# A two-layer decoder trunk on one core: the weights as pairs of half units, twelve Strassen blocks, and the four sums of a block in one buffer

## The chip, the cores and the metric

The kernel runs on one core of a Trainium2 chip. The metric is the device time of one execution in microseconds (us), taken as the median of several runs. Before the change it is 943.9 us.

The core's engines work in parallel, each through its own list of instructions in order: TensorE (PE) multiplies, VectorE (DVE) and ScalarE (ACT) do elementwise work, GpSimd (POOL) and SyncE (SP) here mostly issue transfers (DMAs) from the chip's memory into the core's buffers. An instruction starts when the ones ahead of it on its engine are issued and the results that it needs have been signalled.

## The reference, cut to what matters

Two layers on 256 tokens of width 1024, all in float32. Each has a mixing half and an MLP half; the change concerns the weights of both and the work of the MLP half.

```python
for l in range(2):
    u = rms_norm(h, norm_mix_pre[l])
    q, k, v, xr, yr, pp, gt = split(u @ w_in[l])
    ...                               # attention, recurrence, pooling, gates
    h = h + rms_norm(merged @ w_out[l], norm_mix_post[l])
    m = rms_norm(h, norm_mlp_pre[l])
    y = square(relu(m @ w_mlp_up[l])) @ w_mlp_down[l]     # 1024 -> 4096 -> 1024
    h = h + rms_norm(y, norm_mlp_post[l])
```

## The kernel before, in words

**Split products.** PE multiplies in a format that holds fewer bits than float32. So each float32 operand is split into a high and a low part (`split`, lines L88 to L91: ACT makes the high part by a copy, DVE the low part by a subtraction), and `mm3` (L97 to L100) adds three products: high by high, high by low, low by high. In names, an `h` at the end is a high part and an `l` a low one: `wh` and `wl` of a weight unit, `dh`/`dl`, `sh`/`sl` and `bh`/`bl` of a Strassen block's weights.

**The weight stream.** All weights lie in memory as units of 128 rows by 1024 columns (512 KB) in the order of use. `load_to` has SP load them into a pool of seven buffers (`raws`), `split_to` splits them into the pools `his` and `los` of eight buffers each, `take` hands them to the matmuls. What a buffer's next load waits for is the last reader of what is in it, mostly DVE's subtraction.

**The MLP.** The hidden width of 4096 is cut into 16 blocks of 256. `up(j)` makes a block's hidden values (48 matmuls of 128x256), with ACT doing relu and square (L767, L768). The first ten blocks of a layer are multiplied with `w_mlp_down` by Strassen's scheme: a 2x2 by 2x2 block product with 7 instead of 8 products, each three matmuls of 128x512 (`down`). For this a block's down weights, four tiles of 512 columns here called b12, b21, b11, b22, are used alone (b12, b21 and b22) and in four sums t1 to t4. The sums t1 and t2 come by two POOL transfers (`dma_sums`): L794 brings two tiles into `dsum`, L796 adds a third onto both while it writes. A `dsum` buffer holds the sums of two blocks, there are two such buffers, and `dma_sums` is called for two blocks at a time. DVE makes t3 and t4 from them (L811, L812 in `weight_sums`) in a buffer `t34` of the `raws` pool. `weight_forms` splits t1/t2 and t3/t4 (`sh`, `sl`); `hidden_forms` makes the sums of the hidden values (`sm`, L778 to L781) and their split `xf`. The other six blocks of a layer (`PLAIN`) go without Strassen.

**What sets the order.** The order on each engine is that in which the Python code emits the instructions, but for a few calls that are put ahead by a priority. In the MLP loop `UPS[j]` says how many `up` steps stand in round j, before or in the `down` of block j. `ORDER` does this for the mixing half; `later(RGD, ...)` puts the gates of the recurrence (`rnn_gates`) off by RGD ticks.

Of the kernel before, what the change touches and what calls it, by code (L numbers as in the profile page):

```python
# [9 lines left out]
F32 = mybir.dt.float32  # L10
F32R = mybir.dt.float32r
# [5 lines left out]
L = 2  # L17
D = 1024
T = 256
# [2 lines left out]
EPS = 1e-6  # L22
WINDOWS = (2, 4, 8, 16)
HU_COLS = 1024
HP = 200
WARM = 12
NRAW = 7
NTMP = 28
NHI = 8
MID = 1  # L30
CST = 6
# [27 lines left out]
def trunk(ctx, tc, x, wts, rgw, par, gpost, eye, ctab, out):  # L59
# [6 lines left out]
    los = ctx.enter_context(tc.tile_pool(name="los", bufs=8))  # L66
# [12 lines left out]
    def ttile(shape, dt=F32, nm="t"):  # L79
        return tmp.tile(shape, dt, tag="t", name=nm)  # L80
# [7 lines left out]
    def split(hi, lo, src, scale=None):  # L88
        if scale is None:
            A.activation(hi, src, AF.Copy)  # L90
            V.tensor_tensor(out=lo, in0=src, in1=hi.bitcast(F32), op=ALU.subtract)  # L91
        else:
            A.activation(hi, src, AF.Copy, scale=scale)
            V.scalar_tensor_tensor(out=lo, in0=src, scalar=scale, in1=hi.bitcast(F32),
                                   op0=ALU.mult, op1=ALU.subtract)
# [29 lines left out]
    for i in range(WARM):  # L125
        PE.matmul(wps[:], warm[:, 0:P], warm[:], start=True, stop=True)


    NHU = wts.shape[0]
    st = {"load": 0, "split": 0, "use": 0}  # L130
    raw_t, hu_t = {}, {}

    nstr = NBLK - PLAIN
    pair_at = [[(l + 1) * (NHU // L) - 64 + 6 + 2 * j + 2 * (sum(UPS[:j - 1]) + 1 if j else 0) for j in range(nstr)]
               for l in range(L)]
    half = {i + 1 for at in pair_at for i in at}

    per_layer = NHU // L
    fine = {i + l * per_layer for l in range(L) for i in [*range(FINE[0]), *range(per_layer - 64, per_layer - 64 + FINE[1])]}

    def load_to(n):
        while st["load"] < min(n, NHU):
            i = st["load"]
            r = raws.tile([P, HU_COLS], F32, tag="raw", name=f"raw{i}")
            if i in half:
                nc.sync.dma_start(r[:, 512:1024], wts[i][:, 512:1024])
            else:
                nc.sync.dma_start(r[:], wts[i])
            raw_t[i] = r
            st["load"] += 1  # L150

    def split_to(n):
        while st["split"] < min(n, NHU):
            i = st["split"]
            load_to(i + 1)
            r = raw_t.pop(i)
            wh = his.tile([P, HU_COLS], F32R, tag="wh", name=f"wh{i}")
            wl = los.tile([P, HU_COLS], F32R, tag="wl", name=f"wl{i}")
            parts = 2 if i in fine else 1
            for k in range(parts):  # L160
                sl = slice(k * HU_COLS // parts, (k + 1) * HU_COLS // parts)
                split(wh[:, sl], wl[:, sl], r[:, sl])
            hu_t[i] = (wh, wl)
            st["split"] += 1
        load_to(n + NRAW - 1)

    def take(n):
        split_to(st["use"] + n)
        r = [hu_t.pop(st["use"] + i) for i in range(n)]
        st["use"] += n  # L170
        return r
# [118 lines left out]
    def new_normed(nm):  # L290

        t = acts.tile([P, 2, NC_, T], F32R, tag="both", name=nm, bufs=1)
        return t[:, 0], t[:, 1], t
# [65 lines left out]
        to_features(tt, u, prm[:, l, PG_PRE:PG_PRE + 8], uh, ul)  # L359

    uh, ul, u2 = new_normed("u")
    load_to(2)
    nc.sync.dma_start(h[:, 1, :], x[P:T, :])
    un = [mix_norm(0)]
    split_to(1)
    to_features(0, un[0], prm[:, 0, PG_PRE:PG_PRE + 8], uh, ul, between=lambda: split_to(2))
    split_to(3)
    load_to(CST)
    nc.sync.dma_start(cst[:], ctab)
    un.append(mix_norm(1))  # L370

    for l in range(L):
# [326 lines left out]
                {"pp": unit_pp, "pg": unit_pg, "yr": unit_yr, "xr": unit_xr}[kind](j)  # L699


        gB = gpool.tile([P, D], F32, tag="g", name="gB")
        nc.sync.dma_start(gB[:], gpost[l, 0])
        mix = [[bank([P, 512]) for _ in range(2)] for _ in range(2)]
# [26 lines left out]

        gB = gpool.tile([P, D], F32, tag="g", name="gB2")
        nc.sync.dma_start(gB[:], gpost[l, 1])
        prods, t8s = {}, {}
        zs, forms, wforms = {}, {}, {}

        def up_first():

# [46 lines left out]
            split(f[:, 0, 3:7, :], f[:, 1, 3:7, :], sm[:])  # L785
            forms[j] = f

        def dma_sums(j0):


            t = acts.tile([P, 2, 2, 512], F32, tag="lo", name="dsum")
            js = range(j0, min(j0 + 2, nstr))
            for j in js:
                nc.gpsimd.dma_start(t[:, j - j0], wts[pair_at[l][j]].rearrange("p (b n) -> p b n", b=2))  # L794
            for j in js:
                nc.gpsimd.dma_start(t[:, j - j0], wts[pair_at[l][j] + 1][:, 0:512].unsqueeze(1).to_broadcast([P, 2, 512]),  # L796
                                    accum_op=ALU.add)
                t8s[j] = t[:, j - j0]

        def weight_sums(j):  # L800

            load_to(st["split"] + 2)
            assert st["split"] == pair_at[l][j]
            r0, r1 = raw_t.pop(st["split"]), raw_t.pop(st["split"] + 1)
            st["split"] += 2
            st["use"] += 2
            t12 = t8s.pop(j)
            t34 = raws.tile([P, 2, 512], F32, tag="raw", name="t34")
            w1 = (his.tile([P, HU_COLS], F32R, tag="wh", name="dh"), los.tile([P, HU_COLS], F32R, tag="wl", name="dl"))
            w4 = (ttile([P, 512], F32R, nm="bh"), ttile([P, 512], F32R, nm="bl"))  # L810
            V.tensor_tensor(out=t34[:, 0, :], in0=t12[:, 0, :], in1=r0[:, 512:1024], op=ALU.add)  # L811
            V.tensor_tensor(out=t34[:, 1, :], in0=t34[:, 0, :], in1=r1[:, 512:1024], op=ALU.add)  # L812
            split(w1[0][:], w1[1][:], r0[:])
            split(w4[0][:], w4[1][:], r1[:, 512:1024])
            wforms[j] = [w1, w4, (t12, t34)]
            load_to(st["split"] + NRAW - 2)

        def weight_forms(j):
            for t in wforms[j].pop():
                w = (his.tile([P, HU_COLS], F32R, tag="wh", name="sh"), los.tile([P, HU_COLS], F32R, tag="wl", name="sl"))  # L820
                split(w[0][:], w[1][:], t.rearrange("p b n -> p (b n)"))
                wforms[j].append(w)

        def down(j, part):
            f = forms[j]
            w1, w4, w2, w3 = wforms[j]
            lo_, up_ = slice(0, 512), slice(512, 1024)

            for p, blk, w, cs in ((1, 2, w1, up_), (3, 6, w1, lo_), (2, 0, w4, lo_), (7, 5, w2, lo_), (5, 3, w2, up_),
                                  (6, 4, w3, lo_), (4, 1, w3, up_))[part]:  # L830
# [3 lines left out]
                mm3(prods[p][:], f[:, 0, blk, :], f[:, 1, blk, :], w[0][:, cs], w[1][:, cs], first, last)  # L834

        dma_sums(0)
        up_first()
        dma_sums(2)
        split_to(st["use"] + 2)
        up(2)  # L840
        weight_sums(0)
        split_to(st["use"] + 2)
        weight_forms(0)
        hidden_forms(0)
        nup = 3
        for j in range(nstr):
            if j % 2 and j + 3 < nstr:
                dma_sums(j + 3)
            for i in range(UPS[j]):
                up(nup)  # L850
                nup += 1
                if i == 0 and j + 1 < nstr:
                    weight_sums(j + 1)
                    hidden_forms(j + 1)
                if nup < NBLK:
                    split_to(st["use"] + 2)
# [103 lines left out]
def _layout(i):  # L960
    qc = np.concatenate([np.arange(hd * 64, hd * 64 + 64) for hd in _HEADS])
    units, rg, par, gp = [], [], [], []
    for l in range(L):
# [20 lines left out]
        pairs = [np.stack([np.concatenate([d[c][:, 512:], d[1 - c][:, :512]], 1) for c in range(2)]) for d in dn]  # L984
        units += [_s_units(i["w_mlp_up"][l][:, 0:512])[0], up[2], pairs[0], up[3]]
        nup = 3
        for j in range(nstr):
            for n in range(UPS[j]):
                nup += 1
                if n == 0 and j + 1 < nstr:  # L990
                    units.append(pairs[j + 1])
                if nup < NBLK:
# [14 lines left out]
    f = np.ascontiguousarray  # L1007
    return {
        "x": f(i["x"].reshape(T, D)),
        "wts": f(np.concatenate(units, 0)),  # L1010
        "rgw": f(np.stack(rg)),
        "par": f(np.stack(par, 1)),
        "gpost": f(np.array(gp)),
# [15 lines left out]
```

## Time and profile before

| | us |
|---|---|
| median of 3 runs (lowest, highest) | 943.9 (943.8, 944.44) |
| the profiled execution, its own time | 944.59 |
| its span from the first to the last instruction | 942.8 |
| granted TensorE clock, mean | 0.998 |
| PE busy | 932.3 |
| DVE busy, ACT busy | 750.0, 630.9 |

The rows of a timeline give the start in us, the duration in us, the engine, the line of the kernel, the operation, what it writes and reads, and in brackets how long its engine had been idle ahead of it and what ended that. Grouped rows give the count after an x, then the total in us and the mean in ns. Matmuls are pipelined, so that the distance from one start to the next tells their cost better than the duration of one; for DVE and ACT too, the next instruction may start a little before the last has ended. In the windows of busy time each engine has its busy us and its number of instructions.

### The profile page before, as it was taken

The numbers are of one execution on the slowest core, as the hardware profiler recorded it, in microseconds if no ns is written. First come the engines' busy times: TensorE is split into PE (matmuls) and PEld (weight loads), VectorE is DVE, ScalarE is ACT, GpSimd is POOL, SyncE is SP. The second block draws the span as 40 slices with busy tenths as digits, with TensorE's granted clock in tenths as the row PEclk, the third lists the DMA queues.
The fourth block names the chain that finished last, engine by engine and source line by source line (L and its number), as shares of the span: only waits on it lengthen the run. The fifth ranks groups of instructions, "written<-read, shape, count | busy, mean of one in ns | idle before, by whom it ended". The sixth has DMA issues, their size and how long they took to land.

```text
span 942.8 us, 14266 instructions
## 1 busy us (share of the span) xinstructions
PE 932.3 (99%) x5176; PEld 798.7 (85%) x5176; DVE 750.0 (80%) x1341; ACT 630.9 (67%) x1091; POOL 37.7 (4%) x60
## 2 busy tenths in 40 slices
PE   8999999999999999999999999999999999999997
PEld 5888987888888999998878888888888889999985
DVE  6878886878967987988596788776898598888963
ACT  8665765679837786767475666656896478767741
POOL 0000000000010111100000000000000101110000
PEclk9999999999999999999999999999999999999999
DMA  8765445544776888858457544645438688987621
GB/s 318 277 211 164 157 157 172 191 136 153 239 253 174 271 244 259 257 187 261 136 184 252 171 153 161 197 141 190 162 113 293 180 248 247 269 249 234 225 88 44
DMA packets 57062, 188.96 MB, mean 200 GB/s; under 512 B 6048, under 2 KB 6432, under 8 KB 56992
## 3 DMA queue, kind: packets, MB, share of 16 engines
q1 hardware_dynamic: 48384, 166.92, 52.6%
q0 software_dynamic: 8320, 20.97, 9.9%
q8 instruction: 40, 0.66, 0.3%
q14 instruction: 30, 0.25, 0.1%
q10 hardware_dynamic: 288, 0.17, 0.1%
HBM read 186.99 MB, written 1.05 MB: 199 GB/s over the span
## 4 chain that ended last, share of the span: by engine, by line
PE 98%; ACT 1%; DMA 1%; DVE 0%; issue 0%; SPq 0%; DVEq 0%
PE ps L98 18%; PE ps L99 17%; PE ps L100 17%; PE ps L304 9%; PE ps L341 9%; PE pr L98 6%; PE pr L99 6%; PE pr L100 6%; PE ps L306 5%; PE ps L429 1%; PE ps L477 1%; PE ps L466 1%; PE ps L230 1%; DMA raw<-wts 1%; PE ps L409 0%; PE ps L660 0%
## 5 line engine op out<-in xcount | busy, mean ns | idle before, releaser
L91 DVE TENSOR_TENSOR wl<-raw,wh 128x1024 fp32r<-128x1024 f32 (+1 forms) x304 | 333.5, 1123 | 67.0 <-ACT wh L90 57.7
L90 ACT ACTIVATE wh<-raw 128x1024 fp32r<-128x1024 f32 (+1 forms) x304 | 287.5, 987 | 127.1 <-PE ps L100 49.7
L98 PE MATMUL ps<-m,wh 128*128 128x256 f32 x448 | 126.9, 283 | 0.0
L100 PE MATMUL ps<-m,wl 128*128 128x256 f32 x448 | 126.9, 283 | 0.0
L99 PE MATMUL ps<-m,wh 128*128 128x256 f32 x448 | 126.9, 283 | 0.0
L304 PE MATMUL ps<-u,wh 128*128 128x512 f32 x384 | 96.9, 394 | 0.0
L99 PEld LDWEIGHTS ps<-m,wh 128*128 128x128 f32 x448 | 86.0, 192 | 1.0
L98 PEld LDWEIGHTS ps<-m,wh 128*128 128x128 f32 x448 | 86.0, 192 | 1.0
L100 PEld LDWEIGHTS ps<-m,wl 128*128 128x128 f32 x448 | 86.0, 192 | 0.0
L304 PEld LDWEIGHTS ps<-u,wh 128*128 128x128 f32 x384 | 69.5, 189 | 13.6 <-issue 0.7
L98 PE MATMUL ps<-wh,u 128*128 128x512 f32 x200 | 78.7, 393 | 0.8 <-ACT u L236 0.8
L100 PE MATMUL ps<-wh,u 128*128 128x512 f32 x200 | 78.0, 390 | 0.4 <-DVE u L238 0.4
L99 PE MATMUL ps<-wl,u 128*128 128x512 f32 x200 | 78.1, 391 | 0.0
L306 PEld LDWEIGHTS ps<-u,wl 128*128 128x128 f32 x384 | 52.4, 191 | 3.8
L306 PE MATMUL ps<-u,wl 128*128 128x256 f32 x384 | 53.5, 282 | 0.0
L98 PEld LDWEIGHTS ps<-wh,u 128*128 128x128 f32 x200 | 37.6, 188 | 9.3 <-ACT u L236 1.0
L100 PEld LDWEIGHTS ps<-wh,u 128*128 128x128 f32 x200 | 37.6, 188 | 8.6 <-DVE u L238 0.9
L99 PEld LDWEIGHTS ps<-wl,u 128*128 128x128 f32 x200 | 37.6, 188 | 7.7 <-DVE wl L91 0.4
L341 PE MATMUL ps<-wh,u 128*128 128x512 f32 x176 | 43.3, 394 | 0.0
L448 ACT ACTIVATE pr<-ps,s 128x128 f32<-128x128 f32 (+1 forms) x64 | 25.9, 430 | 25.8 <-DVE s L439 21.3
L341 PEld LDWEIGHTS ps<-wh,u 128*128 128x128 f32 x176 | 32.4, 188 | 7.9 <-ACT wh L90 0.9
L98 PE MATMUL pr<-wh,hid 128*128 128x512 f32 x96 | 37.5, 390 | 0.0
(234 smaller groups left out, 1992.5 us busy)
## 6 DMA issues: line engine op xcount, KB each, us to landing
raw<-wts SPq DMA_DIRECT2D x296, 512.0 KB, 4.6
dsum<-wts POOLq DMA_DIRECT2D x40, 512.0 KB, 6.9
raw<-wts SPq DMA_DIRECT2D x20, 256.0 KB, 5.0
gB<-gpost SPq DMA_DIRECT2D x4, 512.0 KB, 6.9
rg<-rgw SPq DMA_DIRECT2D x8, 256.0 KB, 4.4
out<-h SPq DMA_DIRECT2D x4, 256.0 KB, 2.0
h<-x SPq DMA_DIRECT2D x2, 256.0 KB, 3.3
h<-x SPq DMA_DIRECT2D x1, 512.0 KB, 7.1
```

What stands on the lines that cost most here:

```text
L90: A.activation(hi, src, AF.Copy)
L91: V.tensor_tensor(out=lo, in0=src, in1=hi.bitcast(F32), op=ALU.subtract)
L98: PE.matmul(o, lh, rh, start=start, stop=False, **kw)
L99: PE.matmul(o, lh, rl, start=False, stop=False, **kw)
L100: PE.matmul(o, ll, rh, start=False, stop=stop, **kw)
L230: PE.transpose(banks[c // 4][:, c % 4, :], src[c // 4][:, (c % 4) * P:(c % 4 + 1) * P], ident)
L304: PE.matmul(ps[:], ws[0][c], x2[:, :, c, :], start=c == 0, stop=False)
L306: PE.matmul(ps[:, 0, :], ws[1][c], x2[:, 0, c, :], start=False, stop=c == 7)
L341: PE.matmul(o, xx[:, c, tsl], ww[c], start=(n == 0 and c == 0), stop=(n == 2 and c == 7))
L429: PE.matmul(sc[hd // hp][:, hd % hp, :], qT[a, j // 2][rows, j % 2, blk * P:(blk + 1) * P], kTs[0][rows, a, 0:w], start=True, stop=True)
L448: A.activation(pr[:, j, :], sc[i][:, j, :], AF.Exp, bias=negm[:, hd:hd + 1], accum_out=sums[:, hd:hd + 1])
L466: PE.transpose(ps[:, g, :], g8["p"](4 * b + g)[:, kt * P:(kt + 1) * P], ident)
```

## The change

- A load is now 128 rows by 2048 columns (1 MB): two units side by side. `raws` has four buffers, `his` and `los` four of 2048 columns each. In the MLP a pair is split by one ACT and one DVE instruction of 2048 columns, in the mixing half by two of 1024, and by four of 512 for the first four pairs of a layer and of its MLP.
- A Strassen block's weights are one such row, of which three tiles of 512 columns (b12, b21 and b22 of the list above, 1536 columns) are loaded by SP and split as one piece.
- Twelve instead of ten blocks of a layer go by Strassen, four instead of six without; two `up` steps stand in the first round only.
- The four sums of a block lie in one buffer of 2048 columns: t1 and t2 by POOL's two transfers (now L726 and L727), t3 and t4 added behind them by DVE (now L823, L824). The buffer holds one block, and there are two. They are split as one piece of 2048 columns. `dma_sums(j + 3)` comes after `weight_forms(j + 1)`, and that of the first block ahead of the layer's output projection.
- `rnn_gates` is put off by six ticks instead of four. One temporary buffer fewer (27), and the loads at the program's start are called in pairs.

The core of the diff:

```diff
-NRAW = 7
-NTMP = 28
-NHI = 8
+PU_COLS = 2 * HU_COLS
+NRAW = 4
+NTMP = 27
+NHI = 4
-RGD = 4
-FINE = (8, 8)
-PLAIN = 6
+RGD = 6
+FINE = (4, 4)
+PLAIN = 4
-UPS = (2, 1, 1, 2, 1, 1, 2, 1, 1, 1)
+UPS = (2, 1, 1, 1, 1, 1, 1, 1, 1, 1, 1, 1)
...
+    def split_pair():
+        i = st["split"]
+        load_to(i + 1)
+        r = raw_t.pop(i)
+        wh = his.tile([P, PU_COLS], F32R, tag="wh", name=f"wh{i}")
+        wl = los.tile([P, PU_COLS], F32R, tag="wl", name=f"wl{i}")
+        n = 4 if i in fine else 2 if i % per_layer < per_layer - 32 else 1
...
+        def dma_sums(j):
+            t = acts.tile([P, PU_COLS], F32, tag="lo", name="dsum")
+            w = wts[pair_at[l][j]]
+            t2 = t[:, 0:1024].rearrange("p (b n) -> p b n", b=2)
+            nc.gpsimd.dma_start(t2, w[:, 0:1024].rearrange("p (b n) -> p b n", b=2))
+            nc.gpsimd.dma_start(t2, w[:, 1536:2048].unsqueeze(1).to_broadcast([P, 2, 512]), accum_op=ALU.add)
+            t8s[j] = t
...
         def weight_sums(j):
+            r = raw_t.pop(st["split"])
+            t = t8s[j]
+            V.tensor_tensor(out=t[:, 1024:1536], in0=t[:, 0:512], in1=r[:, 512:1024], op=ALU.add)
+            V.tensor_tensor(out=t[:, 1536:2048], in0=t[:, 1024:1536], in1=r[:, 1024:1536], op=ALU.add)
+            wh = his.tile([P, PU_COLS], F32R, tag="wh", name="dh")
+            wl = los.tile([P, PU_COLS], F32R, tag="wl", name="dl")
+            split(wh[:, 0:1536], wl[:, 0:1536], r[:, 0:1536])
...
         def weight_forms(j):
-            for t in wforms[j].pop():
-                w = (his.tile([P, HU_COLS], F32R, tag="wh", name="sh"), los.tile([P, HU_COLS], F32R, tag="wl", name="sl"))
-                split(w[0][:], w[1][:], t.rearrange("p b n -> p (b n)"))
+            t = t8s.pop(j)
+            wh = his.tile([P, PU_COLS], F32R, tag="wh", name="sh")
+            wl = los.tile([P, PU_COLS], F32R, tag="wl", name="sl")
+            split(wh[:], wl[:], t[:])
...
-            if j % 2 and j + 3 < nstr:
-                dma_sums(j + 3)
             for i in range(UPS[j]):
                 up(nup)
...
             if j + 1 < nstr:
                 weight_forms(j + 1)
+                if j + 3 < nstr:
+                    dma_sums(j + 3)
```

**What moves on DVE.** DVE's rows of one block in the middle of layer 0's MLP; the number in a name tells one buffer's use from another's. Before:

```order
L91 TENSOR_TENSOR bl_3991<-raw125_3836,bh_3990 128x512
L778 TENSOR_TENSOR sm_4000<-z_3561 128x128
L780 TENSOR_TENSOR sm_4000<-sm_4000,z_3561 128x128
L811 TENSOR_TENSOR t34_4110<-dsum_3748,raw128_3914 128x512
L812 TENSOR_TENSOR t34_4110<-t34_4110,raw129_3916 128x512
L91 TENSOR_TENSOR dl_4112<-raw128_3914,dh_4111 128x1024
L91 TENSOR_TENSOR xf_4005<-sm_4000,xf_4005 128x512
L91 TENSOR_TENSOR wl130_4134<-raw130_3998,wh130_4133 128x1024
L91 TENSOR_TENSOR wl131_4138<-raw131_4018,wh131_4137 128x1024
L91 TENSOR_TENSOR sl_4169<-dsum_3748,sh_4168 128x1024
L91 TENSOR_TENSOR sl_4173<-t34_4110,sh_4172 128x1024
```

After:

```order
L823 TENSOR_TENSOR dsum_3682<-dsum_3682,raw65_3685 128x512
L92 TENSOR_TENSOR dl_3846<-raw65_3685,dh_3845 128x1536
L824 TENSOR_TENSOR dsum_3682<-dsum_3682,raw65_3685 128x512
L92 TENSOR_TENSOR xf_3856<-z_3528,xf_3856 128x384
L806 TENSOR_TENSOR sm_3851<-z_3528 128x128
L808 TENSOR_TENSOR sm_3851<-sm_3851,z_3528 128x128
L92 TENSOR_TENSOR wl66_3862<-raw66_3745,wh66_3861 128x2048
L92 TENSOR_TENSOR sl_3887<-dsum_3682,sh_3886 128x2048
L92 TENSOR_TENSOR xf_3856<-sm_3851,xf_3856 128x512
```

The adds that read POOL's sums stand first in a block now, `wl` and `sl` are one row each, and the `xf` of the hidden sums comes behind `sl`.

**What moves on POOL.** The transfers of the sums in layer 0. Before:

```order
L794 DMA dsum_3061<-wts 128x1024 x2
L796 DMA dsum_3061<-wts 128x2x512 x2
L794 DMA dsum_3166<-wts 128x1024 x2
L796 DMA dsum_3166<-wts 128x2x512 x2
L794 DMA dsum_3497<-wts 128x1024 x2
L796 DMA dsum_3497<-wts 128x2x512 x2
```

After:

```order
L726 DMA dsum_3256<-wts 128x1024
L727 DMA dsum_3256<-wts 128x2x512
L726 DMA dsum_3370<-wts 128x1024
L727 DMA dsum_3370<-wts 128x2x512
L726 DMA dsum_3474<-wts 128x1024
L727 DMA dsum_3474<-wts 128x2x512
```

Each buffer is filled for one block by one transfer of either kind, where it was filled for two blocks by two.

**What moves on SP.** The weight loads in the same stretch. Before:

```order
L148 DMA raw124_3816<-wts 128x1024
L146 DMA raw125_3836<-wts 128x512
L148 DMA raw126_3838<-wts 128x1024
L148 DMA raw127_3840<-wts 128x1024
L148 DMA raw128_3914<-wts 128x1024
L146 DMA raw129_3916<-wts 128x512
```

After:

```order
L148 DMA raw59_3373<-wts 128x1536
L148 DMA raw60_3433<-wts 128x2048
L148 DMA raw61_3477<-wts 128x1536
L148 DMA raw62_3537<-wts 128x2048
L148 DMA raw63_3581<-wts 128x1536
```

Four loads per block have become two, of 1 MB for an `up` and of 768 KB for a Strassen block.

More of the change, by code (lines that the diff above doesn't have):

```diff
@@ L126, in trunk @@
         PE.matmul(wps[:], warm[:, 0:P], warm[:], start=True, stop=True)
-    NHU = wts.shape[0]
+    NHU = 2 * wts.shape[0]
     st = {"load": 0, "split": 0, "use": 0}
-    raw_t, hu_t = {}, {}
+    raw_t, hu_t, second = {}, {}, []
+    per_layer = wts.shape[0] // L
     nstr = NBLK - PLAIN
-    pair_at = [[(l + 1) * (NHU // L) - 64 + 6 + 2 * j + 2 * (sum(UPS[:j - 1]) + 1 if j else 0) for j in range(nstr)]
+    pair_at = [[(l + 1) * per_layer - 32 + 4 + j + (sum(UPS[:j - 1]) + (j == 1) if j else 0) for j in range(nstr)]
@@ L135, in trunk @@
                for l in range(L)]
-    half = {i + 1 for at in pair_at for i in at}
-    per_layer = NHU // L
-    fine = {i + l * per_layer for l in range(L) for i in [*range(FINE[0]), *range(per_layer - 64, per_layer - 64 + FINE[1])]}
+    three = {i for at in pair_at for i in at}
+    fine = {i + l * per_layer for l in range(L) for i in [*range(FINE[0]), *range(per_layer - 32, per_layer - 32 + FINE[1])]}
     def load_to(n):
-        while st["load"] < min(n, NHU):
+        while st["load"] < min(n, NHU // 2):
@@ L143, in load_to @@
             i = st["load"]
[L144 to L148, printed above, removed]
+            r = raws.tile([P, PU_COLS], F32, tag="raw", name=f"raw{i}")
+            n_ = 1536 if i in three else PU_COLS
+            step = HU_COLS if i < 2 else n_
+            for c in range(0, n_, step):
+                nc.sync.dma_start(r[:, c:c + step], wts[i][:, c:c + step])
@@ L149, in load_to, with pieces @@
             raw_t[i] = r
             st["load"] += 1
-    def split_to(n):
[L153 to L165, printed above, removed]
+    def split_pair():
[5 more added lines that the diff above has]
+        n = 4 if i in fine else 2 if i % per_layer < per_layer - 32 else 1
+        def pieces(ks):
+            for k in ks:
+                sl = slice(k * PU_COLS // n, (k + 1) * PU_COLS // n)
+                split(wh[:, sl], wl[:, sl], r[:, sl])
+        if i == 0:
+            pieces(range(2))
+            second.append(lambda: pieces(range(2, 4)))
+        else:
+            pieces(range(n))
+        for k in range(2):
+            sl = slice(k * HU_COLS, (k + 1) * HU_COLS)
+            hu_t[2 * i + k] = (wh[:, sl], wl[:, sl])
+        st["split"] += 1
@@ L167, in take @@
+    def split_to(n):
+        while 2 * st["split"] < min(n, NHU):
+            split_pair()
+        load_to((n + 1) // 2 + NRAW - 1)
     def take(n):
+        while st["use"] // 2 in three:
+            st["use"] += 2
         split_to(st["use"] + n)
@@ L361, in trunk @@
     uh, ul, u2 = new_normed("u")
+    load_to(1)
+    nc.sync.dma_start(h[:, 1, :], x[P:T, :])
     load_to(2)
[L363 removed]
     un = [mix_norm(0)]
     split_to(1)
[L366 to L368 removed]
+    to_features(0, un[0], prm[:, 0, PG_PRE:PG_PRE + 8], uh, ul, between=second[0])
+    split_to(4)
+    load_to(3)
     nc.sync.dma_start(cst[:], ctab)
@@ L786, in hidden_forms @@
             forms[j] = f
[L788 to L798, printed above, removed]
@@ L800, in weight_sums @@
         def weight_sums(j):
-            load_to(st["split"] + 2)
+            load_to(st["split"] + 1)
             assert st["split"] == pair_at[l][j]
[L804 to L809, printed above, removed]
@@ new lines, in weight_sums @@
+            st["split"] += 1
+            t = t8s[j]
[4 more added lines that the diff above has]
+            split(wh[:, 0:1536], wl[:, 0:1536], r[:, 0:1536])
+            wforms[j] = [(wh[:, i * 512:(i + 1) * 512], wl[:, i * 512:(i + 1) * 512]) for i in range(3)]
@@ L851, in trunk @@
                 nup += 1
+                if j == 0 and i == 0:
+                    split_pair()
                 if i == 0 and j + 1 < nstr:
```

47 lines of the change are left out of this document (21 added, 26 removed).

## The prediction

> **What bounds the kernel now.** I read the page first: the span, the busy time of the engines, the chain that ended last and the DMA queues.
>
> ```profile
> span 942.8 us, 14266 instructions
> PE 932.3 (99%) x5176; PEld 798.7 (85%) x5176; DVE 750.0 (80%) x1341; ACT 630.9 (67%) x1091; POOL 37.7 (4%) x60
> PE 98%; ACT 1%; DMA 1%; DVE 0%; issue 0%; SPq 0%; DVEq 0%
> q1 hardware_dynamic: 48384, 166.92, 52.6%
> q0 software_dynamic: 8320, 20.97, 9.9%
> ```
>
> TensorE (PE) works 99% of the span and carries 98% of the chain, so time can be won only by taking matmuls away, and lost only where something makes PE wait. Windows over the Strassen stage of layer 0 show that nothing does there now (PE, PEld, DVE, ACT, POOL, granted clock, DMA share, GB/s):
>
> ```profile
> 340.00:360.00 20.00, 20.00 (x134) 18.41 (x133) 17.98 (x28) 14.32 (x20) 3.53 (x4) 1.00 0.88 278
> 360.00:380.00 20.00, 20.00 (x136) 18.54 (x135) 15.52 (x22) 13.96 (x19) 2.34 (x3) 1.00 0.87 240
> ```
>
> PE is busy 20.00 of 20.00 us, but DVE 15.5 to 18.0 and the DMA engines 0.87 to 0.88: both have little to spare if their work is put in another order. The chain of waits gives the beat of a block, from the first matmul of one `down` to that of the next:
>
> ```profile
> 349.90 0.23 PE pr L98
> 354.46 0.23 PE pr L100
> 360.44 0.23 PE pr L98
> ```
>
> A block lasts 360.44 - 349.90 = 10.54 us. The second row is the 21st and last matmul of that `down`: 4.56/20 = 0.228 us for one of 128x512. So `down` (21) takes 4.79 and `up` (48 of 128x256) the other 5.75 us, 0.120 each.
>
> **The change, part by part.** First the gain. A Strassen block does 7 products where the plain form does 8, so two more blocks per layer save 2 products of three 128x512 matmuls, over two layers 2 x 2 x 3 = 12, and 12 x 0.228 = **-2.7 us**. As PE has no gaps, all of it counts if no wait appears.
>
> Next the splits. The grouped lines give DVE and ACT by width, the timeline of DVE the distance from start to start:
>
> ```profile
> L91 DVE TENSOR_TENSOR wl<-raw,wh 128x1024 fp32r<-128x1024 f32 x248 | 297.3, 1222 | 61.8 <-ACT wh L90 52.5 <-PE ps L341 7.8 <-PE ps L306 1.1
> L90 ACT ACTIVATE wh<-raw 128x1024 fp32r<-128x1024 f32 x248 | 256.2, 1064 | 120.8 <-PE ps L100 48.3 <-issue 25.6 <-PE ps L99 17.4
> L90 ACT ACTIVATE wh<-raw 128x512 fp32r<-128x512 f32 x56 | 31.3, 647 | 6.3 <-PE pr L100 3.4 <-PE ps L100 1.3 <-DMA raw<-wts 1.2
> 350.92 1.23 DVE L91 TENSOR_TENSOR sl<-t,sh 128x1024 fp32r<-128x1024 f32 x1 [0.22 <-ACT sh L90]
> 352.06 0.68 DVE L91 TENSOR_TENSOR bl<-raw,bh 128x512 fp32r<-128x512 f32 x1
> 352.66 0.29 DVE L778 TENSOR_TENSOR sm<-z 128x128 f32<-128x128 f32 x1
> 352.86 0.28 DVE L779 TENSOR_TENSOR sm<-z 128x128 f32<-128x128 f32 x1
> 356.41 0.56 DVE L91 TENSOR_TENSOR xf<-z,xf 128x384 fp32r<-128x384 f32 x1
> 356.88 2.36 DVE L91 TENSOR_TENSOR wl<-raw,wh 128x1024 fp32r<-128x1024 f32 x2
> ```
>
> Start to start on DVE: 1.14 us for 1024 columns, 0.60 for 512, 0.47 for 384, 0.20 for 128; another 512 columns cost 0.54, so 1536 take 1.68 and 2048 take 2.22 (2.31 to their end). These two are my extrapolation. A block's DVE work was 4 x 1.14 + dl 1.14 + bl, two adds and xf 4 x 0.60 + xf 0.47 + four small 0.80 = 9.37 us. It becomes 2 x 2.22 + 1.68 + 3 x 0.60 + 0.47 + 0.80 = 9.19: 0.2 us less, worth nothing by itself, since DVE isn't what ends. ACT saves fixed costs in the same way and is hidden under PE. For the weight loads the bytes stay and only the grouping changes; no group of the two lists above shows PE or DVE waiting for a raw load beyond 1.2 us in all, so I put it at 0.
>
> Now what is new: the sums t1 and t2 of a block come by two POOL transfers into a buffer of which there are two. Before, a buffer held t1 and t2 of two blocks, so POOL was four blocks ahead; now it is two ahead. In the order, L726 of block j+3 waits for DVE's `sl` of block j+1, L727 waits until L726 has landed, and DVE's L823 of block j+3 waits for L727. What stands behind L823 on DVE is `dl`, L824, `xf`, three small adds and then `wl` of the next `up`, for which PE waits. So there is a loop over two blocks: a piece C (end of `sl` to L727 landed) and DVE's piece from L823 to the next `sl` end, 0.60 + 1.68 + 0.60 + 0.47 + 3 x 0.20 + 2.22 + 0.20 + 2.31 = 8.68 us. Two blocks are 21.08, so C may be 21.08 - 8.68 = **12.4 us**; beyond it PE waits for the rest once in two blocks.
>
> C comes from the rows of the same transfers, whose form is not changed: first L794's, then L796's landing times, the timeline of POOL, the `sl` ahead of it, and the landing of the one L794 issued at 351.02.
>
> ```profile
> DMA to landing us min/median/max: 4.0/6.2/8.9
> DMA to landing us min/median/max: 6.5/7.7/10.1
> 349.47 1.23 DVE L91 TENSOR_TENSOR sl<-dsum,sh 128x1024 fp32r<-128x1024 f32 x1 [0.81 <-ACT sh L90]
> 351.02 1.12 POOL L794 DMA_DIRECT2D dsum<-wts  x2 [7.72 <-DVE sl L91]
> 358.35 1.21 POOL L796 DMA_DIRECT2D dsum<-wts  x1 [6.21 <-DMA dsum<-wts]
> dsum<-wts POOLq DMA_DIRECT2D x1, 512.0 KB, 6.9
> ```
>
> From the end of `sl` (349.47 + 1.23 = 350.70) to POOL's issue: 0.3 us. From landing (351.02 + 6.9) to the next issue at 358.35: 0.4 us. So C = 0.7 + L726 + L727: with the shortest rows 0.7 + 4.0 + 6.5 = 11.2, with the medians 0.7 + 6.2 + 7.7 = 14.6, with the longest 19.7. Half of the L794 were issued right behind a sibling (1.12 us for the two); the new order has no siblings, for which I take 0.4 off: C = **14.2**. I hold to the medians and not to the shortest since the load streams stay: by the page's rows q1 moves 166.92 MB in 0.526 x 942.8 = 496 us, so a 1 MB transfer (1.05 of these MB) fills all engines for 3.1 us and a 768 KB one for 2.3, and each block still has one of either. Both are freed by DVE in this same loop: L824 frees the 768 KB one about 3.5 us + its wait after `sl` ends, just as L727 begins, and `wl` the 1 MB one before L727 is over.
>
> Passes of the loop: in a layer the blocks 1, 3, 5, 7, 9, 11 make five passes, and the first late sum, that of block 2, a sixth ahead of them. The chain of the even blocks waits at the same DVE and so doesn't add. Two layers: 12 passes x (14.2 - 12.4) = **+21.6 us**. Ends: shortest 0, medians 12 x 2.2 = 26.4.
>
> The other moves. `wl` of an `up` is now one instruction of 2048 and its buffer is single: ACT's `wh` starts when `up` ends (349.9), takes 1.06 + 2 x 0.42 = 1.90 (from the 647 and 1064 ns above), `wl` 2.31, so it is there at about 354.1 while the third matmul of the next `up`, the first that reads it, comes at 354.46 + 0.23 + 0.24 = 354.9. 0.8 us of cover; 0. `rnn_gates` runs two slots later (RGD 6). In these rows its chain lasts from the first tanh to the last split:
>
> ```profile
> 213.38 0.82 ACT L601 ACTIVATE tr<-ps,hb 128x256 f32<-128x256 f32 x2
> 221.99 0.64 ACT L93 ACTIVATE rnh<-ti 128x512 fp32r<-128x512 f32 x1
> ```
>
> that is 9.3 us and 0.7 for DVE's half, 10; in the new order 48 matmuls of 128x512 (10.9 us) lie between the last gates and the first matmul on `rnh`, and the halves of the last gates are read later still. Hidden, with 1 us or more of cover; if it fails, up to 1 us per layer. The first loads of the program carry the same bytes in the same order ahead of `h` and `cst`: 0, within one 512 KB transfer (1.6 us) either way. The four plain blocks at the layer's end have the same work per block as before: 0.
>
> Sum: 944.59 (profiled execution; 942.8 span + 1.8 around it) - 2.7 + 21.6 = 963.5. The median of the runs, 943.9, lies 0.7 below the profiled one, so I say **962.8 us**.
>
> **A rule against the change.** Two windows of the DMA view show how POOL's and SP's transfers share the engines. The first two rows are 353 to 355, POOL nearly alone; the rest is 358 to 360, where the L796 issued at 358.35 landed 10.1 us later:
>
> ```profile
> q0 software_dynamic: 123, 0.47, 76.5%
> q1 hardware_dynamic: 7, 0.02, 3.5%
> ...
> q1 hardware_dynamic: 150, 0.53, 72.8%
> q0 software_dynamic: 35, 0.11, 14.3%
> dsum<-wts POOLq DMA_DIRECT2D x1, 512.0 KB, 10.1
> ```
>
> Beside SP's traffic the same transfer takes 10.1 instead of 6.5 us, and 3.6 is more than one 512 KB load (1.6) can fill. If POOL's rows of 2 KB must each let one of SP's pass, and SP's rows grow from 4 to 8 KB, POOL's transfer can be held for all that SP has there: 11.2 + 2.3 + 3.1 = 16.6 us for C, 12 x 4.2 = 50 us of waits, 991 us. The Trainium skill, page "DMA: Bandwidth & Descriptors", section "Queues, rings and completion order", says that each DMA engine takes turns between the queues that have work for it, one packet at a time. The shares above, summed over 16 engines, neither prove nor refute it.
>
> **The rivals.**
> - *No wait (faster).* The three transfers of a block fall one after the other. Counted from the shortest rows they just can: L726 in the gap behind the 1 MB load, L727 behind the 768 KB one. Then C stays at 11.2 to 12.4 and only the gain is left: 943.9 - 2.7 = 941.2. The two balance at C = 12.4 + 2.7/12 = 12.6. For it: a pair of 4.0 and 6.5 does occur, and no DVE row of before waits for a sum. Against: the medians are 3.4 us longer together, and a late L823 pushes L824, and so the 768 KB load, further into L727.
> - *Heavy collision.* Both loads hold POOL's transfers for most of their time: C above 15.5, 978 to 991. For it: the 10.1 us landing; against: only one L796 in twenty took so long.
> - *The weight split.* `wl` as one piece is later than reckoned, by DVE being behind: each of the 26 `up`s in the loops of both layers waits, at 0.5 us a loss of 13, 954. Against: 0.8 us of cover by the rows.
>
> **How the numbers follow.** Likeliest is the loop with C between 12.8 and 15.5 (946 to 978): chance 0.45, at 962.8. Heavy collision 0.18, weight split 0.06, no wait 0.24, and 0.07 for C near balance. About 0.2% (1.9 us) is what a measurement here tells from no change. Faster takes the no-wait case and a little of the balance: 0.25; same the rest of it: 0.06; slower 0.69. The range goes from the no-wait case, 941, to C = 15.8, that is 943.9 - 2.7 + 12 x 3.4 = 982, leaving out most of the heavy case.
>
> **What would show it.** Right: in the trace after, DVE sits idle before L823 with a DMA `dsum<-wts` as releaser, in about every second block, some 1 to 3 us; PE's idle time is named after `wl` or `wh` in the `up` matmuls; the first `down` rows of two successive blocks lie 11 to 12 us apart instead of 10.54; L726 and L727 land in 5 to 6 and 7 to 9 us. Wrong: PE busy 20.00 of 20.00 in the MLP windows, L823 without a wait, 12 PE matmuls fewer and nothing else. Weight split: PE waits for `wl` while DVE was not held at L823. My forecast fails first if the transfers of a block fall into step and land near 4.0 and 6.5.

## The result and the profile after

The changed kernel takes **961.78 us** (median; 958.71 to 963.52), the kernel before 944.17 in the same comparison: a ratio of 1.0184, 95% interval 1.0171 to 1.0196. That is 17.6 us slower; 962.8 was forecast. The profiled execution is the shortest of the four, 958.71 us with a span of 956.9, 14.1 more than before; all that follows on where the time went is read from it.

The page of the changed kernel:

```profile
span 956.9 us, 13605 instructions
PE 935.2 (98%) x5164; PEld 800.8 (84%) x5164; DVE 761.2 (80%) x1301; ACT 627.9 (66%) x1027; POOL 45.0 (5%) x68
PE 83%; DVE 5%; DMA 5%; issue 4%; ACT 2%; POOL 0%; DVEq 0%; SPq 0%; POOLq 0%
```

PE has 12 instructions fewer (5176 to 5164). In the chain that ended last its share fell from 98% to 83%; DVE and a DMA took its place. Waits by pair, and the landing times of L726 and L727 (engine, line, what it waited for: us in total, times, longest):

```profile
DVE dsum L823 <- DMA dsum<-wts: 28.5, 13, 5.8
PE ps L101 <- DVE wl L92: 10.6, 5, 4.1
DMA to landing us min/median/max: 3.5/5.6/7.3
DMA to landing us min/median/max: 5.3/6.5/9.1
```

The first row is DVE's wait for POOL's sums before L823, in 13 of the 24 blocks; the second is PE's wait for `wl` behind that. PE's waits aren't spread over the blocks: four gaps make up nearly all. The timelines around the first one show each step, first the `sl` that frees the buffer, then POOL, then DVE, then PE:

```profile
387.16 2.29 DVE L92 TENSOR_TENSOR sl<-dsum,sh 128x2048 fp32r<-128x2048 f32 x1
389.76 0.59 POOL L726 DMA_DIRECT2D dsum<-wts  x1 [3.57 <-DVE sl L92]
396.24 1.19 POOL L727 DMA_DIRECT2D dsum<-wts  x1 [5.89 <-DMA dsum<-wts]
405.24 0.69 DVE L823 TENSOR_TENSOR dsum<-dsum,raw 128x512 f32<-128x512 f32 x1 [4.80 <-DMA dsum<-wts]
405.85 1.75 DVE L92 TENSOR_TENSOR dl<-raw,dh 128x1536 fp32r<-128x1536 f32 x1
409.19 2.29 DVE L92 TENSOR_TENSOR wl<-raw,wh 128x2048 fp32r<-128x2048 f32 x1
408.16 0.28 PE L100 MATMUL ps<-m,wh 128*128 128x256 f32 x1
411.53 0.54 PE L101 MATMUL ps<-m,wl 128*128 128x256 f32 x1 [3.09 <-DVE wl L92]
```

`sl` ended at 389.45, L726 landed at 395.8, and L727, issued at 396.24, at 405.21. C, the time from the end of `sl` to the landed sums, was 15.8 us where 12.4 were allowed. DVE stood still for 4.80 us, `wl` came at 411.5, and PE had waited 3.4 us since its second matmul. Windows of the MLP stage (PE, PEld, DVE, ACT, POOL, granted clock, DMA share, GB/s):

```profile
340.00:360.00 20.00, 20.00 (x133) 18.36 (x132) 16.82 (x17) 14.16 (x14) 3.57 (x4) 1.00 0.92 277
400.00:420.00 20.00, 16.91 (x104) 15.65 (x103) 13.63 (x19) 8.53 (x9) 2.41 (x4) 0.91 0.85 253
411.60:414.00 2.40, 2.40 (x11) 2.40 (x12) 2.40 (x3) 1.42 (x3) 0.00 (x0) 0.50 1.00 309
```

Most windows are like the first, full as before. In the one with the gap the granted clock, too, is down: 0.50 right behind the gap.

The account of the profiled executions, from the distances between the starts of matmuls: in the Strassen stages of the two layers 5.5 and 10.5 us are lost against the usual spacing, 0.3 and 0.2 before; of these 15.5 us more, the four gaps (3.2, 2.0, 1.5 and 4.3 us) make 11.0 and the slow clock behind two of them 4.3. Less 2.7 for the 12 matmuls that is 12.8 of the 14.1; the other 1.3 are lost in small pieces outside these stages.

### The profile page after: what moved, and what is told of

It is laid out like the page before. It is cut to its first block, busy times and chain, and to the rows that moved or that the text cites. A ratio compares the mean times of both kernels' runs of the same rounds, so it can differ in the third digit from the quotient of the medians.

```text
span 956.9 us, 13605 instructions
## 1 busy us (share of the span) xinstructions
PE 935.2 (98%) x5164; PEld 800.8 (84%) x5164; DVE 761.2 (80%) x1301; ACT 627.9 (66%) x1027; POOL 45.0 (5%) x68
## 4 chain that ended last, share of the span: by engine, by line
PE 83%; DVE 5%; DMA 5%; issue 4%; ACT 2%; POOL 0%; DVEq 0%; SPq 0%; POOLq 0%
PE ps L99 16%; PE ps L101 15%; PE ps L100 15%; PE ps L320 9%; PE ps L357 8%; PE ps L322 4%; DMA dsum<-wts 4%; PE pr L99 4%; PE pr L100 3%; PE pr L101 3%; DVE wl L92 2%; PE ps L446 1%; PE ps L494 1%; DVE sl L92 1%; PE ps L483 1%
## 5 line engine op out<-in xcount | busy, mean ns | idle before, releaser
L91 ACT ACTIVATE wh<-raw 128x1024 fp32r<-128x1024 f32 (+2 forms) x268 | 273.6, 1067 | 181.7 <-PE ps L100 77.9
L92 DVE TENSOR_TENSOR wl<-raw,wh 128x1024 fp32r<-128x1024 f32 (+2 forms) x268 | 321.1, 1221 | 69.6 <-ACT wh L91 58.1
L101 PE MATMUL ps<-m,wl 128*128 128x256 f32 x448 | 129.2, 288 | 10.6 <-DVE wl L92 10.6
L99 PE MATMUL ps<-m,wh 128*128 128x256 f32 x448 | 128.7, 287 | 0.0
L100 PE MATMUL ps<-m,wh 128*128 128x256 f32 x448 | 128.5, 287 | 0.0
L99 PEld LDWEIGHTS ps<-m,wh 128*128 128x128 f32 x448 | 87.7, 196 | 1.6 <-ACT z L795 0.5
L100 PEld LDWEIGHTS ps<-m,wh 128*128 128x128 f32 x448 | 87.5, 195 | 0.9
L320 PEld LDWEIGHTS ps<-u,wh 128*128 128x128 f32 x384 | 69.3, 189 | 13.5 <-issue 0.7
L92 DVE TENSOR_TENSOR sl<-dsum,sh 128x2048 fp32r<-128x2048 f32 x24 | 54.9, 2286 | 0.3 <-ACT sh L91 0.2
L91 ACT ACTIVATE sh<-dsum 128x2048 fp32r<-128x2048 f32 x24 | 45.9, 1913 | 13.4 <-DVE dsum L824 6.8
L99 PEld LDWEIGHTS ps<-wh,u 128*128 128x128 f32 x200 | 37.5, 188 | 10.6 <-PE ps L494 1.6
L101 PEld LDWEIGHTS ps<-wh,u 128*128 128x128 f32 x200 | 37.5, 188 | 8.7 <-DVE u L254 0.9
L92 DVE TENSOR_TENSOR dl<-raw,dh 128x1536 fp32r<-128x1536 f32 x24 | 42.1, 1754 | 3.4 <-ACT dh L91 3.4
```

What stands on the lines that cost most here:

```text
L99: PE.matmul(o, lh, rh, start=start, stop=False, **kw)
L100: PE.matmul(o, lh, rl, start=False, stop=False, **kw)
L101: PE.matmul(o, ll, rh, start=False, stop=stop, **kw)
L320: PE.matmul(ps[:], ws[0][c], x2[:, :, c, :], start=c == 0, stop=False)
```

## The experiments

The theory was the loop of the prediction: the sums are two blocks ahead, and `sl` to landed sums (C) takes longer than the loop of two blocks allows. Rivals: the split of `wl` as one piece; SP's loads or their 8 KB rows as such; the twelve blocks.

**Sums four ahead.** Pairs of blocks share a buffer of t1 and t2 again, t3 and t4 are written over the raw tile, and the sums are split in two pieces of 1024:

```diff
-            t = acts.tile([P, PU_COLS], F32, tag="lo", name="dsum")
+            t = acts.tile([P, 2, HU_COLS], F32, tag="lo", name="dsum")
...
+            V.tensor_tensor(out=r[:, 512:1024], in0=t[:, 0:512], in1=r[:, 512:1024], op=ALU.add)
+            V.tensor_tensor(out=r[:, 1024:1536], in0=r[:, 512:1024], in1=r[:, 1024:1536], op=ALU.add)
...
+            if j % 2 and j + 3 < nstr:
+                dma_sums(j + 3)
```

> The changed kernel with the sums fetched as before, two blocks to a buffer and so up to four blocks ahead; t3 and t4 are written over the raw tiles after these are split (no more memory), and the sums are split in two pieces of 1024. 1 MB loads, wl in one piece and twelve blocks stay. If the loop is the cause: no wait before the adds (now L828), no gap of PE, 941 to 942.5 us, faster than both kernels. If the weight split or the 1 MB loads are the cause: 955 to 963. If the raw buffers held longer now run short: waits for raw loads and 943 to 950.

942.55 us, 0.9985 of before (0.9975 to 0.9994). `wl` is still one piece of 2048, the loads are 1 MB, the blocks twelve; PE's waits in the MLP are gone:

```profile
400.00:420.00 20.00, 20.00 (x131) 18.32 (x131) 18.14 (x24) 13.69 (x15) 2.43 (x2) 1.00 0.94 296
```

So the split in one piece isn't the cause, nor are the loads without the loop.

**No MLP loads.** SP's loads away, the loop left:

```diff
+            if i % per_layer >= per_layer - 26:
+                raw_t[i] = keep[0]
+                st["load"] += 1
+                continue
```

> The changed kernel with SP's weight loads of the last 26 pairs of each layer left out (all Strassen blocks but the first, and the plain blocks, work on one pair that is already there; the values are wrong, the instructions on PE, ACT, DVE and POOL the same). If SP's loads are what holds POOL's transfers, L726 and L727 land in about 4.0 and 6.5 us in every block, 11.3 us for the way from sl to the sums, under the 12.4 that the loop allows: no wait before L823 above 1 us, no gap of PE, 941 to 943 us. If POOL's transfers are slow by themselves (their own queue, the accumulation), their times stay at up to 7 and 9 us and the time at 955 to 963.

943.23 us (0.9995; 0.9986 to 1.0005). The two transfers (here L731 and L732) land in

```profile
DMA to landing us min/median/max: 3.5/3.9/6.9
DMA to landing us min/median/max: 5.2/5.4/7.5
```

and C is 9.6 to 10.6 us in all 20 blocks that go through the loop, against 9.7 to 16.8 (median 12.6, mean 12.8) in the changed kernel. SP's loads are what makes C long. That the loop still runs here and loses nothing shows that its limit lies above 10.6.

**No third tile.**

```diff
-            nc.gpsimd.dma_start(t2, w[:, 1536:2048].unsqueeze(1).to_broadcast([P, 2, 512]), accum_op=ALU.add)
```

> The changed kernel without POOL's second transfer (L727): the third tile of t1 and t2 is left out, so the sums are wrong, while every split, add and matmul stays. If the loop over two blocks is the cause (the sums are only two blocks ahead, and L726 plus L727 take longer than the loop allows): the way from the end of sl to the sums shrinks from 11 to 17 us to about 6, DVE no longer waits before L823, PE has no gap in the MLP, and the time is 943.9 - 2.7 = 941 to 943 us. If the weight split as one piece is the cause: PE goes on waiting for wl, 955 to 963. If the row length or the number of blocks costs something by itself: between, 945 to 955.

A miss: 952.52 us (1.0096; 1.0078 to 1.0114). The lists of instructions are sorted by a scheduler when the program is built, which the text ahead of the prediction did not say, and with the shorter way it had put the adds of a block ahead of the `sl` of the block before. With that `sl` queued behind the add, the loop closes over one block instead of two. POOL's and DVE's timelines:

```profile
380.07 0.54 POOL L726 DMA_DIRECT2D dsum<-wts  x1 [10.42 <-DVE sl L92]
383.93 0.69 DVE L822 TENSOR_TENSOR dsum<-dsum,raw 128x512 f32<-128x512 f32 x1 [1.54 <-issue]
388.28 2.28 DVE L92 TENSOR_TENSOR sl<-dsum,sh 128x2048 fp32r<-128x2048 f32 x1
390.97 0.53 POOL L726 DMA_DIRECT2D dsum<-wts  x1 [10.36 <-DVE sl L92]
```

10.9 us from one L726 to the next: 3.9 to the add, 4.35 to `sl`, 2.28 for it, 0.4 to POOL. (The row of L822 names no releaser; the sums landed at 383.86, just ahead of it.) A block of 10.54 can't hold that, and most blocks are late by some tenths.

**The same, order held.** DVE's adds tied behind that `sl`:

```diff
+            last[:] = [split(wh[:], wl[:], t[:]).ins]       # in weight_forms
...
+            with tc.issue_after(last[0]) if last else nullcontext():
+                V.tensor_tensor(...)                         # the two adds
```

> The run without POOL's second transfer again, now with DVE's two adds held behind the sl of the block before, so that DVE's order is row for row that of the changed kernel (in the first run the scheduler had put the adds of a block ahead of that sl, which made a loop of one block: 4.4 us for L726 plus 6.6 us of DVE, 11.0 instead of 10.54). Third tile still left out. If the loop over two blocks is the cause: the way from sl to the sums is 4 to 7 us of the 12.4 allowed, no wait of DVE at the adds, no gap of PE, 941 to 943. If the weight split in one piece is the cause: 955 to 963.

942.87 us (0.9986; 0.9976 to 0.9995), C 3.8 to 5.2 us. A shorter C alone, under the changed kernel's order, removes the loss.

**`wl` in halves.**

```diff
-        n = 4 if i in fine else 2 if i % per_layer < per_layer - 32 else 1
+        n = 4 if i in fine else 2
```

> The changed kernel with the weights of an up split as two pieces of 1024 columns instead of one of 2048, as in the kernel before. If the loop is the cause, DVE waits before L823 as it does now and PE behind it: 957 to 965 us, like the changed kernel. If the weight split as one piece is the cause, PE gets the first half earlier and its waits for wl go: 941 to 946.

1046.29 us (1.1112; 1.1052 to 1.1171), outside both expectations, by the same sorting: here the add that waits for the sums of the next block stands ahead of `sl`, with C at its full length, so a block lasts about C + 4 us. DVE's wait for the sums rose from 28.5 to 132.6 us:

```profile
DVE dsum L823 <- DMA dsum<-wts: 132.6, 20, 11.0
399.43 0.69 DVE L823 TENSOR_TENSOR dsum<-dsum,raw 128x512 f32<-128x512 f32 x1 [10.97 <-DMA dsum<-wts]
401.36 2.28 DVE L92 TENSOR_TENSOR sl<-dsum,sh 128x2048 fp32r<-128x2048 f32 x1
```

**The same, order held** by the tie shown above:

```diff
+        n = 4 if i in fine else 2
...
+            with tc.issue_after(last[0]) if last else nullcontext():
```

> The weights of an up split in two pieces of 1024 again, with the adds held behind the sl of the block before, as in the changed kernel (in the first run the scheduler had put the add that waits for POOL ahead of that sl, so that the loop closed over one block). If the loop over two blocks is the cause: 955 to 965, with DVE's waits at the adds and PE's behind them like those of the changed kernel. If the weight split in one piece is the cause: 941 to 946.

968.4 us (1.0239; 1.0202 to 1.0275): the gain that the rival promised isn't there, and it is somewhat more than the loop was expected to give. C is 13.9 on average there, 1 us above the changed kernel's.

**Rows of 4 KB.**

```diff
-            step = HU_COLS if i < 2 else n_
-            for c in range(0, n_, step):
+            for c in range(0, n_, HU_COLS):
```

> The changed kernel with SP's 1 MB loads issued as two of 1024 columns (rows of 4 KB instead of 8; 1024 + 512 for a Strassen block), the adds held behind sl as in the changed kernel. If POOL's rows of 2 and 4 KB take turns with SP's row by row, halving SP's rows shortens what POOL waits: the landing times of L726 and L727 fall from 5.6 and 6.5 (median) towards 5 and 6, the long ones (over 8 us) go, and the time falls to 945 to 955. If only the bytes count, the times and 957 to 963 us stay.

966.28 us (1.0249; 1.0217 to 1.0281). L726 and L727 landed not sooner but later (medians 5.8 and 7.2, C 13.9 on average against 12.8). So shorter rows don't free POOL's transfers. With the run without MLP loads it follows that it is the loads themselves that hold them; whether by their bytes or by the moments at which they start, no run here separates.

**Adds behind `dl`.**

```diff
             split(wh[:, 0:1536], wl[:, 0:1536], r[:, 0:1536])
+            hidden_forms(j)
+            V.tensor_tensor(...)                             # the two adds, moved here
```

> The changed kernel with the two adds emitted behind dl and the split of the hidden values, still ahead of wl; sums two blocks ahead as before. In the order, dl (1.68 us) and xf (0.47) now stand ahead of the first add, so DVE can be late there by 2.1 us more before wl is late: the loop allows 14.5 us instead of 12.4. Of the 24 ways from sl to the sums in the changed kernel 4 are longer than that (15.1 to 16.8 us). If the loop is the cause: 943 to 950 us, with one to four gaps of PE. If it is not: 957 to 963.

964.02 us (1.0207; 1.0153 to 1.026), a miss. The room grew, but C grew with it: ten of the 20 are at 15 us or more (median 14.2, up to 18.0) where four were. The second add is the last reader of the raw tile, and so it is what lets SP start the next 768 KB load. Moved later, it puts off that load, and L727 lands later too. Whether the one makes the other stays open: in the ten long passes the load starts 0.2 to 2.7 us ahead of L727, in the changed kernel's 20 passes anywhere from 3.2 us ahead to 1.4 us behind, so these starts alone don't tell long passes from short ones (L727 in this run):

```profile
DMA to landing us min/median/max: 5.4/7.1/10.9
```

**Twelve blocks in the kernel before**, and nothing else:

```diff
-PLAIN = 6
+PLAIN = 4
-UPS = (2, 1, 1, 2, 1, 1, 2, 1, 1, 1)
+UPS = (2, 1, 1, 1, 1, 1, 1, 1, 1, 1, 1, 1)
```

> The kernel before with twelve Strassen blocks (PLAIN 4, two ups in the first round only) and nothing else of the change: units of 512 KB, splits of 1024 columns, sums of two blocks to a buffer and up to four ahead. If the twelve blocks are worth their 12 matmuls and the loss sits in the two-deep sums: 943.9 - 2.7 = 941 to 942 us, PE without a gap. If a steady row of blocks with one up each (no round with two ups to catch up in) is itself the cause: waits of PE, 945 to 960.

941.19 us (0.9969; 0.9956 to 0.9981): 2.9 us faster, the 12 matmuls. It beats both kernels, and all variants here.

**Two ahead in the kernel before**, ten blocks; a buffer holds the sums of one block:

```diff
-                t8s[j] = t[:, j - j0]
+            t8s[j] = t[:, 0]
...
-            if j % 2 and j + 3 < nstr:
-                dma_sums(j + 3)
...
             if j + 1 < nstr:
                 weight_forms(j + 1)
+                if j + 3 < nstr:
+                    dma_sums(j + 3)
```

> The kernel before with one block instead of two to a dsum buffer, so that the sums are two blocks ahead instead of four; 512 KB loads, ten blocks and all else as before. DVE's piece of the loop is here from L806 to the sl of t1 and t2, about 7.1 us by the rows of the kernel before, so the way from sl to the sums may take 21.1 - 7.1 = 14.0 us, and the three rounds with two ups give 5.8 us more each. If the two-deep sums lose time by themselves: waits of DVE at L806 and some gaps of PE, 945 to 953. If they do so only with 1 MB loads or in twelve blocks: 943.5 to 944.5.

944.4 us (1.0002; 0.9993 to 1.0011): no loss, though C was 13.5 to 19.3 us, 16.0 on average, and DVE waited

```profile
DVE t L806 <- DMA dsum<-wts: 21.6, 9, 4.1
```

The rounds with two `up`s had given the room: over ten rounds of which three last 16.3 us, two blocks take 24.5 on average, which leaves 17.4 for C beside the 7.1 of DVE's piece.

**The same with twelve blocks**, two `up`s in the first round only:

```diff
-PLAIN = 6
+PLAIN = 4
-UPS = (2, 1, 1, 2, 1, 1, 2, 1, 1, 1)
+UPS = (2, 1, 1, 1, 1, 1, 1, 1, 1, 1, 1, 1)
```

> The kernel before with sums two blocks ahead and twelve blocks (two ups in the first round only); 512 KB loads, splits of 1024, buffers and all else as before. In the run with ten blocks the way from sl to the sums was 13.5 to 19.3 us, 16.0 on average; the loop allows 2 x 10.54 - 7.1 = 14.0 us in rounds with one up, but 17.4 on the average of ten rounds of which three have two ups (16.3 us). With twelve blocks only the first round has two. If the loop alone decides: 12 passes x (16.0 - 14.0) = 24 us less 2.7, about 965, within 950 to 975. If the 1 MB loads or the split of 2048 columns are needed for the loss: 941 to 943.

959.18 us (1.0178; 1.0121 to 1.0235), with 512 KB loads and splits of 1024. C is as long as with ten blocks (16.2 on average), but the room is gone; DVE's wait is 36.4 us, and PE has gaps now:

```profile
DVE t L806 <- DMA dsum<-wts: 36.4, 14, 5.8
PE pr L98 <- ACT xf L90: 5.5, 3, 2.7
PE pr L100 <- DVE xf L91: 4.5, 5, 0.9
```

In this order of instructions the late engine reaches PE through `xf` and not through `wl`. This settles the cause: two-deep sums and rounds with a single `up` lose the time together; each alone loses nothing, and neither the 1 MB loads nor the 2048 split is needed for it.

**PE gaps by length.** In the run with the sums four ahead ACT gets extra copies, so that it, and PE behind it, is late by a rising time:

```diff
+        for _ in range(extra):
+            A.activation(r[:, 0:512], r[:, 0:512], AF.Copy)
```

> The run with the sums four ahead, in which ACT copies a raw tile's first 512 columns onto themselves 6, 7, 8, ... 16 times ahead of one weight split in every second round, so that PE gets gaps of rising length. In the changed kernel PE's clock was granted at half for 3 to 5 us after the gaps of 3.3 and 4.3 us, and stayed full after those of 2.0 and 1.5. If the length of the gap decides: full clock after every gap up to some length between 2.0 and 3.3 us, half after every longer one, for longer after a longer gap. If it was chance or the DMA traffic: no such order. Time about 960 to 980, no verdict from it.

977.64 us, a single run. The clock stayed full after the shortest of the five gaps and was halved after the four longer ones, as expected if the length decides; two other runs don't keep to that order. Both are read in the last section.

## Why the prediction was right, point by point

- *The gain of 2.7 us.* Right: 2.9 measured alone.
- *The loop.* Right as mechanism, in its place and its releaser: DVE idle before L823 for `dsum<-wts`, PE waiting for `wl`. The price was 21.6 us; the medians give 17.6 + 2.7 less about 1.3 for the other moves, 19.0. That the forecast of 962.8 came within about 1 us of the median, 961.78, is in part luck, as the next two points show.
- *Its inner numbers were less right than the sum.* C was put at 14.2 in every pass; it was 12.6 in the median and ran from 9.7 to 16.8. By the mean of 12.8 the formula would have given 12 x 0.4 = 5 us. What the mean hides is that a wait comes from the passes that are too long, and the short ones give nothing back: 11 of 20 were above 12.4, and these 11 together by 21 us. Four of them, 15.1 to 16.8 us, opened the four gaps. Three more, 13.8 to 14.2, came in the block right behind a gap, when DVE was late by more than that already, and cost nothing: the chains of the even and the odd blocks hide each other's waits, as the prediction had it. The last four were over by 0.1 to 1.1 us, and the cover of `wl` took that up but for 0.4 us. And 4.3 us are a cost that wasn't in the sum: the clock behind two of the gaps.
- *The pattern* was wrong: a wait of 1 to 3 us in every second block, and 11 to 12 us per block, were forecast. There were four gaps of 1.5 to 4.3 us and otherwise nearly all blocks had the old length.
- *The medians of before as price.* L796's 7.7 came down to 6.5 (7 to 9 were forecast), L794's 6.2 to 5.6. The argument that SP's loads keep them long was right (no MLP loads: 3.9 and 5.4).
- *No wait* was the rival of the other sign. With the loop in place it comes when C is cut short, by leaving out SP's loads or the third tile.
- *Heavy collision* was the case in 3 of 20 blocks (C above 15.5), not in all. The rule that the prediction named for it, the Trainium skill, page "DMA: Bandwidth & Descriptors", section "Queues, rings and completion order" (engines take turns packet by packet), would have shorter rows of SP help POOL only if a packet is one row, as the profile counts them; the page gives a packet several descriptors. With 4 KB rows C got 1 us longer. The rule is not refuted by that, but it doesn't price this kernel.
- *The weight split* fell: in one piece with the sums four ahead PE never waits for `wl`.
- *Moves put at nothing.* Nearly: 1.3 us together, of them 0.5 in a wait for a `wh` between the layers. About as much lies between 942.55 (sums four ahead) and 941.19 (twelve blocks in the kernel before); no run takes these moves one by one.

## What to carry to other kernels

Where a buffer is filled by a DMA and freed by the engine that waits for it, write down the loop: the way of the data, the engine's piece from the wait to the freeing, and the number of periods that the buffers span; its room is the difference, and work in a round that has nothing to do with the loop (the second `up` here) is room too. Price such a wait by the spread of the transfer's time and not by its middle, since only the passes that are too long cost anything. And look at the built order after every edit, the experiments' too: a scheduler that moves one add ahead of the instruction that frees its buffer cost 10 us in one run and 78 in another.

## What the runs showed of the hardware that was not expected

A gap of PE can cost more than its length. In the changed kernel the gap of 2.0 us (854.66 to 856.79) was followed by the full clock, those of 3.2 and 4.3 us (to 411.53 and to 894.30) by half the clock:

```profile
857.00:860.00 3.00, 3.00 (x26) 3.00 (x26) 2.73 (x2) 1.28 (x3) 0.55 (x1) 1.00 0.99 144
894.30:896.00 1.70, 1.70 (x8) 1.70 (x9) 1.70 (x2) 1.49 (x3) 0.00 (x0) 0.50 1.06 339
```

The start-to-start distance of a 128x256 matmul was 0.213 instead of 0.120 us for 3.3 and 5.3 us, a cost of 1.6 and 2.7 us. In the run with gaps made by ACT, too, it was the longer ones that half the clock followed. Each of its gaps below was followed by a few matmuls and some by a second pause of 0.6 us:

```profile
447.40:451.00 3.60, 3.24 (x21) 2.69 (x22) 3.60 (x3) 3.60 (x4) 0.00 (x0) 1.00 0.30 68
851.90:856.20 4.30, 3.97 (x15) 3.34 (x16) 4.30 (x4) 4.19 (x4) 1.13 (x2) 0.60 0.45 143
935.00:941.00 6.00, 5.70 (x21) 4.81 (x22) 5.87 (x4) 5.60 (x5) 0.00 (x0) 0.50 0.39 137
```

After 2.0 + 0.6 us (the first row) the clock stayed full; after 2.3 + 0.6 and after 3.0 + 0.6 it was halved for 3.4 us; after 3.6 and after 5.8 the matmuls ran at half for 5.4 and 6.4.

The length of the gap alone doesn't decide, though. The first two rows below are from the run with the adds behind `dl`: behind a gap of 2.2 us the clock is halved. The other two are from the run with rows of 4 KB: behind a gap of 2.7 us it stays full.

```profile
912.70:916.11 3.41, 1.43 (x11) 1.18 (x10) 3.41 (x5) 3.38 (x5) 0.00 (x0) 1.00 0.62 216
916.11:919.52 3.41, 3.41 (x19) 3.41 (x18) 3.41 (x5) 2.83 (x3) 0.00 (x0) 0.50 0.96 401
431.34:434.75 3.41, 1.88 (x10) 1.41 (x8) 3.41 (x7) 2.24 (x2) 1.19 (x1) 1.00 0.32 77
434.75:438.16 3.41, 2.41 (x20) 2.41 (x21) 3.41 (x4) 2.50 (x4) 0.00 (x0) 1.00 0.87 255
```

These windows are cut where the clock can change. In every trace here its changes lie whole steps of 3.413 us apart; in the changed kernel they come at 411.60, 415.02, 892.88 and 899.71, that is 1, 140 and 2 steps from one to the next. What went with half the clock is a step in which PE did little: 1.43 of 3.41 us in the first row, a share of 0.42, against 1.88, or 0.55, in the third, where the longer gap is spread over two steps. Over all steps of all traces that began at the full clock, those with PE busy for 0.42 or less were followed by half the clock and those with 0.48 or more by the full one; in between both occurred (PE's ends are modelled, so these shares are rough). So a gap of 2 to 3 us may or may not cost extra, by where it falls among the steps, and that the five gaps above came in order of length is partly chance.

The Trainium skill, page "TensorE: Matmul & The Clock Gate", section "Part 1: The HAM clock gate", gives half rate after an idle window of about 3.4 us and a similar time of work until the full rate is back. The traces agree on the length of the window; they differ in that it need not be idle throughout, as the first row shows.
